# Third layer's attention: outputs built transposed with the values as the stationary operand, and GpSimd's tile work moved to VectorE and ScalarE

## The chip, the cores and the metric

The kernel runs on one core of a Trainium2 chip. A core has TensorE (PE, with the loading of its stationary operand shown as PEld), VectorE (DVE), ScalarE (ACT), GpSimd (POOL) and SyncE (SP), which issues transfers. Each engine takes its own instructions strictly in the order in which the program issued them, and semaphores order the engines among each other. The metric is the device time of one execution in microseconds, lower is better; a time of this kernel is compared by the median of several runs.

## The reference, cut to what matters

The program is three transformer layers on 256 tokens of width 1024. The third layer's attention is a sparse one with 16 heads of 64 in 4 groups; queries of a group share keys and values. With 256 tokens the selected blocks and the window both come to plain causal attention over their own keys and values, so that what the kernel must compute for each head is

```python
s = einsum('qd,kd->qk', q, k_slc) * scale      # selected branch, causal
o_slc = softmax(s) @ v_slc
s = einsum('qd,kd->qk', q, k_win) * scale      # window branch, causal
o_win = softmax(s) @ v_win
p_cmp = softmax(q @ k_cmp.T * scale)           # 15 compressed keys
o_cmp = p_cmp @ v_cmp
o = g[0] * o_cmp + g[1] * o_slc + g[2] * o_win # gates, one per head and branch
x = x + concat(o) @ od_w_out
```

with `q`, the keys and the values projected by `od_w_in` and the keys and queries rotated (rope). All of it is float32. Where a plain float32 product would cost too much, the kernel splits an operand into a rounded part `hi` and a remainder `lo` and uses three products.

## The kernel before, in words

The third layer's attention is the stage in `nsa`, run by `pace(nsa(...), od_fill(), 1.0)`. Its order is written out by hand (`manual_schedule`), so each engine sees the instructions as the program issues them.

`nsa` is a software pipeline over 28 units. A unit with `j` is a block of 128 queries (`j` 0 or 1) for one head of a group (`j` = 1, `hp` = 1) or two (`j` = 0, `hp` = 2), for both branches `s` (selected, window); `par` says whether the heads lie in the lower or the upper 64 partitions. Four units `a` to `d` without `j` are the compressed branch of a group. In step t the program issues `weigh` of the unit two steps back, `turn` of the unit three back, `scores` of the unit t, `values` of the unit four back and `out` of the unit five back, then `pace` takes from `od_fill` about one part of weights.

- `scores`: PE forms the scores (lines 2553 to 2555) in PSUM, DVE takes the row maxima (2557), ACT the exponentials with their sums (2563).
- `weigh`: DVE takes the reciprocal of the sums, multiplies it by the gates (2578, 2579) and scales the probabilities, one `tensor_scalar` for each head and branch (2584).
- `turn`: PE transposes the four 128-column blocks of probabilities (2595); ACT or DVE copies them out of PSUM as `pT` (2598, 2600).
- `values`: PE multiplies with the probabilities `pT` as the stationary operand and 64 columns of values `vsw` as the moving one (2619). The output has queries on its partitions; a bank holds a group's four heads and both query blocks. In the last unit of a query block ACT copies 256 columns to `Onsa` (2523).
- `out`: PE transposes `Onsa` (2628), and `split` writes `mix`: ACT the `hi` part (303), DVE the `lo` part (307).

`od_fill` supplies the layer's own projections (weights in float32 are loaded to `raw`, split by `parts`: `whi` by ACT at line 303 and `wlo` by DVE at line 307 or by POOL at line 305, then multiplied at lines 296 to 298 by `mm3`), the rope of queries and keys, the two compress steps, and the first half of the output projection (`out_pair`). The split of a part is issued up to six parts before its product. From the first step of `nsa` on, `K.pool_share = range(6)` sends every `wlo` of the stage to POOL. POOL also makes the remainders of the rotated queries and keys (`stack`, line 2296; `twice`, line 2305), the shifted upper half of the two compress inputs and the sum with their position term (`upper`, lines 2340 and 2348), and two small products of the compressed branch (2545, 2575). Before step t a unit waits (in program order) until the queries of its group are there, so that `pace` issues as much of `od_fill` as is needed; that makes some steps long.

Of the kernel before, what the change touches and what calls it, by code (L numbers as in the profile page):

```python
# [2290 lines left out]
def stack(K, dst, rows, src, low=None):  # L2291


    nc = K.nc
    nc.scalar.activation(dst[rows], src[rows], AF.Copy)
    nc.gpsimd.tensor_tensor(dst[HIP if rows == LOP else LOP], src[rows], dst[rows].bitcast(F32), op=OP.subtract)


def twice(K, hi, lo, rows, src):
# [4 lines left out]
    for o in (LOP, HIP):  # L2304
        nc.gpsimd.tensor_tensor(lo[o], src[rows], hi[rows].bitcast(F32), op=OP.subtract)


def od_blocks(K, pool, hT, T, done):
# [24 lines left out]
    def halves(c0, m, roped, flag):  # L2333
# [3 lines left out]
        def upper():  # L2337
            dst = T["XC"][m]
            for g in range(0, 4, 2):
                nc.gpsimd.tensor_scalar(dst[HIP, g:g + 2, :255], dst[LOP, g:g + 2, 1:], 1.0, None, op0=OP.mult)  # L2340
# [4 lines left out]
            for g in range(4):  # L2345
                a = dst[:, g, :]
                win = bass.AP(tensor=a.tensor, offset=a.offset, ap=[list(a.ap[0]), [2, 16], [16, 15]])
                nc.gpsimd.tensor_tensor(tmp[:, :, g, :], win, bc(pe, 2, 15), op=OP.add)
# [126 lines left out]
def nsa(K, pool, T, mix, done):  # L2475

    nc = K.nc
# [32 lines left out]
    pos, mixed = {}, []  # L2510

    def into(u):

        new = u.b not in pos
        if new:
            pos[u.b] = bank(K)
        return pos[u.b], new

    def ends(u):
        u.O = {}  # L2520
        for j in u.ends:
            u.O[j] = pool.tile([128, 256], F32, name="Onsa", bufs=2)
            nc.scalar.activation(u.O[j], pos[u.b][:, j * 256:j * 256 + 256], AF.Copy)

    def scores(u):
        b = u.b
        if u.j is None:
# [17 lines left out]
            nc.gpsimd.tensor_tensor(u.sv, u.sv, bc(mv, 2, 16), op=OP.subtract)  # L2545
# [21 lines left out]
    def weigh(u):  # L2567
        if u.j is None:
# [6 lines left out]
            nc.gpsimd.tensor_tensor(u.sv, u.sv, bc(dv, 2, 16), op=OP.mult)  # L2575
# [4 lines left out]
        for ii in range(u.hp):  # L2580
            h = 4 * u.b + 2 * (u.i0 + ii) + u.par
            for s in range(2):
                q = (ii * 2 + s) * u.nk
                nc.vector.tensor_scalar(u.pr[:, q:q + u.nk], u.pr[:, q:q + u.nk], den[:, u.j, h, s:s + 1], None, op0=OP.mult)  # L2584
# [18 lines left out]
    def values(u):  # L2603
        if u.j is None:
            po, new = into(u)
            for j in range(2):
                nc.tensor.matmul(po[:, j * 256:j * 256 + 256], u.pT[:, j * 128:j * 128 + 128],
                                 T["vbd"][:, u.b].rearrange("p h d -> p (h d)"), start=new and j == 0, stop=bool(u.ends),
                                 skip_group_check=True)
            ends(u)  # L2610
            return 0.9
        j, g = u.j, u.b
        po, new = into(u)
        for ii in range(u.hp):
            o = j * 256 + (2 * (u.i0 + ii) + u.par) * 64
            for s in range(2):
# [240 lines left out]
```

## Time and profile before

| | |
|---|---|
| device time, median of 3 runs | 1319.19 us (1313.31 to 1320.64) |
| profiled execution: its own time, and its span | 1319.46 us, 1317.7 us |
| busy over the span: PE, PEld | 1246.6 us (95%), 1076.8 us (82%) |
| DVE, ACT, POOL | 921.5 us (70%), 738.0 us (56%), 295.1 us (22%) |
| mean granted clock of TensorE | 0.97 |
| attention of the third layer | about 949 to 1105 us of the span |

A busy PE is not yet PE at its peak, since matmuls overlap and their ends are modelled: what counts is how far apart their starts are. A busy share is a mean over stages with different limits, so that the stage has to be looked at by itself. A granted clock of 1.0 is 2.4 GHz and of 0.5 is 1.2 GHz; a mean between them is a mix.

### The profile page before, as it was taken

The page shows a single profiled execution, that of the slowest core. Times are in us where ns is not written, and L with a number is a line of the kernel's source. Part 1 is how long each engine was busy: PE and PEld are TensorE (multiplying, and loading weights), DVE is VectorE, ACT ScalarE, POOL GpSimd, SP SyncE. Part 2 cuts the span into 40 slices and gives each one's busy share as a digit, 9 for nine tenths or more (in the row PEclk, how much of TensorE's full clock was granted, in tenths as well). Part 3 has the DMA queues.
Part 4 walks back from the last instruction along what each step waited for, and adds up shares of the span by engine and source line. Part 5 has one row for each costly group of instructions (what it writes and reads, how often), then busy time and mean ns, then how long its engine had stood idle before and what let it go on. Part 6 is the DMA issues. An engine that isn't in the chain of part 4 may idle for free.

```text
span 1317.7 us, 21124 instructions
## 1 busy us (share of the span) xinstructions
PE 1246.6 (95%) x7798; PEld 1076.8 (82%) x7798; DVE 921.5 (70%) x1711; ACT 738.0 (56%) x1545; POOL 295.1 (22%) x332
## 2 busy tenths in 40 slices
PE   7998999799999999989999999999999999999997
PEld 7687997677777777768876799988888777999986
DVE  4778535699999999986866555555468676655562
ACT  6854313489888886865444344454455554544451
POOL 7133005534343432311020000000048321000000
PEclk9999967899999999999999999999999999999999
DMA  8321006669999999737321365565252313555560
GB/s 276 112 96 49 2 1 176 210 236 346 368 325 323 321 355 310 257 110 224 129 65 33 113 192 191 184 224 186 70 159 65 129 33 96 179 176 177 190 224 33
DMA packets 173292, 228.65 MB, mean 174 GB/s; under 512 B 10577, under 2 KB 152225, under 8 KB 173185
## 3 DMA queue, kind: packets, MB, share of 16 engines
q1 hardware_dynamic: 171680, 223.77, 50.7%
q0 software_dynamic: 1504, 3.49, 1.1%
q8 instruction: 63, 1.03, 0.3%
q14 instruction: 45, 0.36, 0.1%
HBM read 226.18 MB, written 1.05 MB: 172 GB/s over the span
## 4 chain that ended last, share of the span: by engine, by line
PE 47%; DVE 4%; ACT 2%; issue 1%; DMA 1%; POOL 0%; DVEq 0%; POOLq 0%; ACTq 0%
PE ps L298 13%; PE ps L296 13%; PE ps L297 13%; PE ps L2619 1%; DMA raw<-in_ev_w_in_dram 1%; DVE pr L2584 1%; PE ps L2595 1%; PE ps L1880 1%; DVE wlo L307 1%; PE ps L2554 1%; PE ps L2197 1%; PE ps L2093 1%; PE ps L2437 1%; ACT whi L303 1%; PE ps L2025 1%
## 5 line engine op out<-in xcount | busy, mean ns | idle before, releaser
L307 DVE TENSOR_TENSOR wlo<-raw,whi 128x512 fp32r<-128x512 f32 (+2 forms) x712 | 514.4, 773 | 75.4 <-ACT whi L303 73.9
L303 ACT ACTIVATE whi<-raw 128x512 fp32r<-128x512 f32 (+1 forms) x821 | 470.7, 624 | 113.6 <-PE ps L298 32.7
L296 PE MATMUL ps<-hTh,whi 128*128 128x256 f32 (+1 forms) x1032 | 301.4, 292 | 1.2 <-ACT whi L303 1.2
L298 PE MATMUL ps<-hTh,wlo 128*128 128x256 f32 (+1 forms) x1032 | 292.3, 283 | 0.2 <-DVE wlo L307 0.2
L297 PE MATMUL ps<-hTl,whi 128*128 128x256 f32 (+1 forms) x1032 | 291.8, 283 | 0.0
L305 POOL TENSOR_TENSOR wlo<-raw,whi 128x512 fp32r<-128x512 f32 x109 | 165.7, 1532 | 302.3 <-ACT whi L303 230.3
L296 PEld LDWEIGHTS ps<-hTh,whi 128*128 128x128 f32 (+1 forms) x1032 | 196.6, 190 | 6.0 <-issue 3.2
L297 PEld LDWEIGHTS ps<-hTl,whi 128*128 128x128 f32 (+1 forms) x1032 | 197.2, 191 | 2.7 <-issue 2.4
L298 PEld LDWEIGHTS ps<-hTh,wlo 128*128 128x128 f32 (+1 forms) x1032 | 195.9, 190 | 0.4 <-DVE wlo L307 0.4
L271 POOL TENSOR_TENSOR nrs<-nv,mhalf 128x1 f32<-128x1 f32 x10 | 5.6, 556 | 469.0 <-DVE nv L1678 469.0
L297 PE MATMUL ps<-wlo,xh 128*128 128x512 f32 x256 | 102.0, 398 | 3.3 <-DVE wlo L307 2.9
L296 PE MATMUL ps<-whi,xh 128*128 128x512 f32 x256 | 103.9, 406 | 0.0
L298 PE MATMUL ps<-whi,xl 128*128 128x512 f32 x256 | 101.0, 395 | 0.0
L303 ACT ACTIVATE hh<-sl 128x512 fp32r<-128x512 f32 x20 | 12.6, 631 | 115.0 <-DVE sl L1770 115.0
L1770 DVE TENSOR_TENSOR sl<-sl,ps 128x512 f32<-128x512 f32 x20 | 13.7, 687 | 88.9 <-PE ps L298 88.9
L296 PE MATMUL ps<-whi,hTh 128*128 128x256 f32 (+3 forms) x192 | 62.6, 327 | 9.5 <-ACT hTh L303 5.5
L297 PE MATMUL ps<-wlo,hh 128*128 128x512 f32 x176 | 69.6, 395 | 0.0
L296 PE MATMUL ps<-whi,hh 128*128 128x512 f32 x176 | 69.3, 394 | 0.0
L298 PE MATMUL ps<-whi,hTl 128*128 128x256 f32 (+3 forms) x192 | 61.7, 322 | 1.3 <-DVE hTl L307 1.3
L297 PE MATMUL ps<-wlo,hTh 128*128 128x256 f32 (+3 forms) x192 | 61.5, 321 | 1.2 <-POOL wlo L305 0.8
L297 PEld LDWEIGHTS ps<-wlo,xh 128*128 128x128 f32 x256 | 48.1, 188 | 16.8 <-DVE wlo L307 7.2
L298 PEld LDWEIGHTS ps<-whi,xl 128*128 128x128 f32 x256 | 48.1, 188 | 11.0
(882 smaller groups left out, 2251.5 us busy)
## 6 DMA issues: line engine op xcount, KB each, us to landing
raw<-in_w_gate_dram SPq DMA_DIRECT2D x64, 512.0 KB, 6.0
raw<-in_w_up_dram SPq DMA_DIRECT2D x64, 512.0 KB, 6.8
raw<-in_w_down_dram SPq DMA_DIRECT2D x32, 1024.0 KB, 7.2
raw<-in_ffn_w_gate_dram SPq DMA_DIRECT2D x22, 1024.0 KB, 5.2
raw<-in_ffn_w_up_dram SPq DMA_DIRECT2D x22, 1024.0 KB, 5.7
raw<-in_ffn_w_down_dram SPq DMA_DIRECT2D x22, 1024.0 KB, 5.0
raw<-in_ev_w_in_dram SPq DMA_DIRECT2D x11, 1024.0 KB, 5.4
raw<-in_od_w_in_dram SPq DMA_DIRECT2D x10, 1024.0 KB, 5.2
```

Of the source, the lines that this page charges most:

```text
L296: nc.tensor.matmul(ps, lh, rh, start=start, stop=False, **kw)
L297: nc.tensor.matmul(ps, lh, rl, start=False, stop=False, **kw)
L298: nc.tensor.matmul(ps, ll, rh, start=False, stop=stop, **kw)
L303: K.nc.scalar.activation(hi, src, AF.Copy)
L305: K.nc.gpsimd.tensor_tensor(lo, src, hi.bitcast(F32), op=OP.subtract)
L307: K.nc.vector.tensor_tensor(lo, src, hi.bitcast(F32), op=OP.subtract)
L1770: nc.vector.tensor_tensor(sl, sl, pu, op=OP.mult)
L1880: nc.tensor.matmul(p2, c[f"R{d}"], z.rearrange("p b t -> p (b t)"), start=True, stop=True)
L2025: nc.tensor.matmul(p[:, bb * nk:bb * nk + nk], T["iqT"][rows[par], b0 + bb, j * 128:j * 128 + 128], ikT[rows[par], :nk], start=True, stop= ...
L2093: nc.tensor.matmul(o, T["qrT"][r, i, js], krT[r, :nk], start=False, stop=False, skip_group_check=True)
L2197: nc.tensor.matmul(oo, qb[rows[m], h0 + i, js], kb[rows[m], h0 + i, :nk], start=i == 0, stop=False, skip_group_check=True)
L2437: nc.tensor.matmul(p[:, :60], w1[:, i, :], tmp[:, i].rearrange("p g n -> p (g n)"), start=i == 0, stop=i == 15)
```

## The change

`values` swaps the operands: 64 columns of `vsw` are stationary and the transposed probabilities move, 128 columns for a unit with `j` = 1 and 256 for one with `j` = 0. The output has the head's 64 value dimensions on partitions, the lower 64 for the heads with `par` 0, the upper 64 for those with `par` 1. A unit with `par` 0 keeps its `pT`; the unit with `par` 1 issues the products of both, in turn. A group's bank then holds what `mix` needs, so that `Onsa`, its copy and the transposes in `out` are gone, `out` splits from the bank itself, and the pipeline is one step shorter. The compressed branch is turned round in the same way.

Nothing of the layer's tile work is left on POOL: `wlo` in this stage, `stack`, `twice`, the position term and the two small products are issued on DVE, the shifted copy on ACT, and of `weigh`'s scalings those of the window branch (`s` = 1) go to ACT.

```diff
@@ stack, twice @@
-    nc.gpsimd.tensor_tensor(dst[HIP if rows == LOP else LOP], src[rows], dst[rows].bitcast(F32), op=OP.subtract)
+    nc.vector.tensor_tensor(dst[HIP if rows == LOP else LOP], src[rows], dst[rows].bitcast(F32), op=OP.subtract)
...
-        nc.gpsimd.tensor_tensor(lo[o], src[rows], hi[rows].bitcast(F32), op=OP.subtract)
+        nc.vector.tensor_tensor(lo[o], src[rows], hi[rows].bitcast(F32), op=OP.subtract)
@@ upper @@
-                nc.gpsimd.tensor_scalar(dst[HIP, g:g + 2, :255], dst[LOP, g:g + 2, 1:], 1.0, None, op0=OP.mult)
+                nc.scalar.activation(dst[HIP, g:g + 2, :255], dst[LOP, g:g + 2, 1:], AF.Copy)
...
-                nc.gpsimd.tensor_tensor(tmp[:, :, g, :], win, bc(pe, 2, 15), op=OP.add)
+                nc.vector.tensor_tensor(tmp[:, :, g, :], win, bc(pe, 2, 15), op=OP.add)
@@ nsa @@
-    def ends(u):
-        u.O = {}
-        for j in u.ends:
-            u.O[j] = pool.tile([128, 256], F32, name="Onsa", bufs=2)
-            nc.scalar.activation(u.O[j], pos[u.b][:, j * 256:j * 256 + 256], AF.Copy)
...
-            nc.gpsimd.tensor_tensor(u.sv, u.sv, bc(mv, 2, 16), op=OP.subtract)
+            nc.vector.tensor_tensor(u.sv, u.sv, bc(mv, 2, 16), op=OP.subtract)
...
-            nc.gpsimd.tensor_tensor(u.sv, u.sv, bc(dv, 2, 16), op=OP.mult)
+            nc.vector.tensor_tensor(u.sv, u.sv, bc(dv, 2, 16), op=OP.mult)
...
-                nc.vector.tensor_scalar(u.pr[:, q:q + u.nk], u.pr[:, q:q + u.nk], den[:, u.j, h, s:s + 1], None, op0=OP.mult)
+                o, d = u.pr[:, q:q + u.nk], den[:, u.j, h, s:s + 1]
+                if s:
+                    nc.scalar.activation(o, o, AF.Copy, scale=d)
+                else:
+                    nc.vector.tensor_scalar(o, o, d, None, op0=OP.mult)
...
         j, g = u.j, u.b
-        po, new = into(u)
-        for ii in range(u.hp):
-            o = j * 256 + (2 * (u.i0 + ii) + u.par) * 64
-            for s in range(2):
-                for b in range(j + 1):
-                    bb = (ii * 2 + s) * (j + 1) + b
-                    nc.tensor.matmul(po[:, o:o + 64], u.pT[:, bb * 128:bb * 128 + 128], vsw[:, b, s, g * 64:g * 64 + 64],
-                                     start=new and ii + s + b == 0, stop=s == 1 and b == j, skip_group_check=True)
-        ends(u)
-        return 0.9
+        if u.par == 0:
+            held[g] = u.pT
+            return 0.0
+        pts = [t.rearrange("p (i s b q) -> p i s b q", i=u.hp, s=2, b=j + 1) for t in (held.pop(g), u.pT)]
+        o = po[:, u.i0:u.i0 + u.hp, u.js]
+        for s in range(2):
+            for b in range(j + 1):
+                for par, r in enumerate(rows):
+                    nc.tensor.matmul(o[r], vsw[:, b, s, g * 64:g * 64 + 64], pts[par][:, :, s, b], start=new[par],
+                                     stop=s == 1 and b == j, skip_group_check=True)
+                    new[par] = False
+        return 0.55
 
     def out(u):
         for j in u.ends:
-            p = bank(K)
-            for k in range(2):
-                nc.tensor.transpose(p[:, k * 128:k * 128 + 128], u.O[j][:, k * 128:k * 128 + 128], K.ident)
             ks, t = slice(2 * u.b, 2 * u.b + 2), slice(j * 128, j * 128 + 128)
-            split(K, mix[0][:, ks, t], mix[1][:, ks, t], p[:, :256].rearrange("p (k t) -> p k t", k=2))
+            split(K, mix[0][:, ks, t], mix[1][:, ks, t], pos[u.b][:, :, t])
...
-    lags = ((weigh, 2), (turn, 3), (scores, 0), (values, 4), (out, 5))
+    lags = ((weigh, 2), (turn, 3), (scores, 0), (values, 4), (out, 4))
...
-        if not t:
-            K.pool_share = range(6)
```

## Rows read from the trace of the kernel before

**Rows 1.** Busy time in stretches of the stage: PE, PEld, DVE, ACT, POOL, clock, DMA.

```profile
988.00:1001.00 13.00, 11.37 (x69) 9.26 (x70) 12.50 (x25) 6.88 (x25) 11.06 (x10) 0.87 0.29 83
...
sum 169.00, PE 160.80 PEld 134.13 DVE 122.62 ACT 92.03 POOL 68.56; mean PE 12.37 PEld 10.32 DVE 9.43 ACT 7.08 POOL 5.27
```

**Rows 2.** PE's instructions grouped, 955 to 1115 us: busy us, mean ns.

```profile
L2619 PE MATMUL ps<-vsw,pT 128*128 128x64 f32 x192 | 24.2, 269 | 0.0
```

**Rows 3.** Chain that ended last, in order of time: start, us, what.

```profile
995.98 0.84 PE ps L2619 x8
...
1084.21 0.44 PE ps L2628 x4
```

**Rows 4.** PE in order of time, layer two's output projection (L2155 alternates halves).

```profile
717.34 1.09 PE L2155 MATMUL ps<-olT,wuv 128*64 128x128 f32 x16
...
727.59 0.40 PE L297 MATMUL ps<-wlo,mxh 128*128 128x512 f32 x1
727.92 0.66 PE L2155 MATMUL ps<-olT,wuv 128*64 128x128 f32 x8
728.50 0.50 PE L298 MATMUL ps<-whi,mxl 128*128 128x512 f32 x1
728.84 0.40 PE L296 MATMUL ps<-whi,mxh 128*128 128x512 f32 x1
729.07 0.40 PE L297 MATMUL ps<-wlo,mxh 128*128 128x512 f32 x1
```

**Rows 5.** DVE's instructions grouped by shape, 949 to 1115 us.

```profile
L307 DVE TENSOR_TENSOR wlo<-raw,whi 128x512 fp32r<-128x512 f32 x30 | 21.7, 775 | 12.0 <-ACT whi L303 11.9
L2584 DVE TENSOR_SCALAR pr<-pr,den 128x256 f32<-128x256 f32 x32 | 18.3, 612 | 0.9
L2584 DVE TENSOR_SCALAR pr<-pr,den 128x128 f32<-128x128 f32 x32 | 12.7, 459 | 0.3
```

**Rows 6.** POOL's instructions grouped by shape, same stretch.

```profile
L305 POOL TENSOR_TENSOR wlo<-raw,whi 128x512 fp32r<-128x512 f32 x24 | 30.6, 1293 | 29.7 <-ACT whi L303 23.5 <-issue 6.0
L2305 POOL TENSOR_TENSOR KTl<-kf,KTh 64x512 fp32r<-64x512 f32 x8 | 11.8, 1476 | 26.8 <-ACT KTh L2303 26.5
```

**Rows 7.** DVE in order of time, four places of the stage.

```profile
984.17 0.67 DVE L307 TENSOR_TENSOR wlo<-raw,whi 128x512 fp32r<-128x512 f32 x1
984.77 1.27 DVE L2557 TENSOR_REDUCE mx<-ps 128x2 f32<-128x512 f32 x2
...
988.36 1.63 DVE L2584 TENSOR_SCALAR pr<-pr,den 128x256 f32<-128x256 f32 x2
...
1010.30 0.69 DVE L2557 TENSOR_REDUCE mx<-ps 128x2 f32<-128x512 f32 x1 [1.76 <-PE ps L2555]
...
1013.95 0.69 DVE L2557 TENSOR_REDUCE mx<-ps 128x2 f32<-128x512 f32 x1 [0.19 <-PE ps L2555]
...
1053.10 0.61 DVE L2584 TENSOR_SCALAR pr<-pr,den 128x256 f32<-128x256 f32 x2
...
1094.31 3.92 DVE L2584 TENSOR_SCALAR pr<-pr,den 128x128 f32<-128x128 f32 x4
```

**Rows 8.** POOL in order of time, around two of those places.

```profile
988.51 2.65 POOL L305 TENSOR_TENSOR wlo<-raw,whi 128x512 fp32r<-128x512 f32 x2 [6.01 <-issue]
...
1092.99 4.97 POOL L305 TENSOR_TENSOR wlo<-raw,whi 128x512 fp32r<-128x512 f32 x4 [4.79 <-ACT whi L303]
```

**Rows 9.** Who waited for whom, 955 to 1110 us: total, times, longest.

```profile
ACT pr L2563 <- DVE mx L2557: 20.0, 17, 3.8
...
ACT s L2546 <- POOL s L2545: 8.0, 4, 3.6
...
PE ps L2595 <- DVE pr L2584: 7.1, 8, 1.5
```

**Rows 10.** ACT in order of time, one unit's exponentials and the split behind them.

```profile
986.84 0.47 ACT L2563 ACTIVATE pr<-ps,mx 128x256 f32<-128x256 f32 x1
...
987.75 0.62 ACT L303 ACTIVATE whi<-raw 128x512 fp32r<-128x512 f32 x1
```

More of the change, by code (lines that the diff above doesn't have):

```diff
@@ L2509, in nsa @@
             [u for u in g if u.j == 1][-1].ends = (1,)
-    pos, mixed = {}, []
+    pos, fresh, mixed, held = {}, {}, [], {}
     def into(u):
[L2514 to L2517, printed above, removed]
-    def ends(u):
-        u.O = {}
-        for j in u.ends:
-            u.O[j] = pool.tile([128, 256], F32, name="Onsa", bufs=2)
-            nc.scalar.activation(u.O[j], pos[u.b][:, j * 256:j * 256 + 256], AF.Copy)
+        if u.b not in pos:
+            pos[u.b] = bank(K).rearrange("p (i t) -> p i t", i=2)
+            fresh[u.b] = [True, True]
+        return pos[u.b]
     def scores(u):
@@ L2603, in values @@
     def values(u):
+        po = into(u)
+        new = fresh[u.b]
         if u.j is None:
-            po, new = into(u)
[L2606 to L2609, printed above, removed]
-            ends(u)
-            return 0.9
-        j, g = u.j, u.b
@@ L2613, in values @@
-        po, new = into(u)
-        for ii in range(u.hp):
-            o = j * 256 + (2 * (u.i0 + ii) + u.par) * 64
-            for s in range(2):
-                for b in range(j + 1):
-                    bb = (ii * 2 + s) * (j + 1) + b
-                    nc.tensor.matmul(po[:, o:o + 64], u.pT[:, bb * 128:bb * 128 + 128], vsw[:, b, s, g * 64:g * 64 + 64],
-                                     start=new and ii + s + b == 0, stop=s == 1 and b == j, skip_group_check=True)
-        ends(u)
-        return 0.9
+            for i in range(2):
+                nc.tensor.matmul(po[:, i], T["vbd"][:, u.b, 2 * i:2 * i + 2].rearrange("p h d -> p (h d)"), u.pT,
+                                 start=new[0] and i == 0, stop=bool(u.ends), skip_group_check=True)
@@ new lines, in values @@
+            new[:] = False, False
+            return 0.5
+        j, g = u.j, u.b
+        if u.par == 0:
[9 more added lines that the diff above has]
+                    new[par] = False
@@ L2632, in out @@
                 mixed.append(("mix", u.b))
-        return 0.2 * len(u.ends)
-    lags = ((weigh, 2), (turn, 3), (scores, 0), (values, 4), (out, 5))
+        return 0.0
+    lags = ((weigh, 2), (turn, 3), (scores, 0), (values, 4), (out, 4))
     yield lambda: done.issuperset(("ks", "kw"))
-    for t in range(len(units) + 5):
+    for t in range(len(units) + 4):
         if t < len(units):
             yield lambda: units[t].b in done and (units[t].j is not None or "cmp" in done)
-        if not t:
-            K.pool_share = range(6)
@@ L2642, in nsa @@
         done.update(mixed)
         yield sum(f(units[t - d]) or 0.0 for f, d in lags if 0 <= t - d < len(units))
-    K.pool_share = ()
     done.update(mixed)
```

## The prediction, as it was made before the result

> **What bounds the kernel now.** I read the page first: PE is busy nearly throughout, so time can leave only where PE's own work shrinks or PE stands still. Next the busy time by stretches of the stage that the change touches [rows 1]: of 169 us PE is busy 160.8, DVE 122.6, ACT 92.0 and POOL 68.6. PE bounds the stage as a mean, but not everywhere: from 988 to 1001 DVE is busy 12.5 of 13 us, PE only 11.4, and PE's granted clock falls to 0.87, a mix of 2.4 and 1.2 GHz. The list of waits says for what PE stands still: for DVE's scaling of the probabilities, 7.1 us in eight times [rows 9].
>
> Then DVE in order of time, beside POOL. Two scalings of 256 columns take 0.61 us at 1053, when POOL has nothing; at 988 they take 1.63, at 1094 four of half that length take 3.92, both while POOL works on `wlo` [rows 7, 8]. So DVE's scalings, on average 612 and 459 ns [rows 5], are long because of POOL. The Trainium skill (SBUF — State Buffer, "SBUF: two separate sides") says that GpSimd and a VectorE instruction that reads two SBUF tensors, or runs in a two-port mode, hold a shared port pair exclusively. The trace agrees with that by the 1.63 and 3.92 us.
>
> **PE's work.** The old `values` is 192 instructions [rows 2] (each float32 product counts as two) in 24 runs of eight at 0.84 us, so 20.2 us; `out` has four runs of four transposes at 0.44, so 1.8 [rows 3]. Together 22.0.
>
> The new form does not occur in this stage, but layer two's L2155 has it: 128 rows, 64 output columns, lower and upper half in turn, 128 moving columns. Sixteen of them span 1.09 us and eight 0.66 [rows 4]: eight more cost 0.43, or 0.054 each, half of what a lone stream of 128 columns in two passes would be if the halves did not overlap. Of the 12 new runs, eight (`j` = 1) have 16 instructions of 128 columns, 0.86 us; four (`j` = 0) have 8 of 256 columns, by length 0.108 each and also 0.86. Sum 10.4.
>
> Each run also leaves the full-array form and comes back to it. In layer two, starts of full 512-column products lie 0.23 us apart (728.84 to 729.07); with a run of eight between them 0.91 (727.59 to 728.50), so 0.91 − 0.23 − 0.43 = 0.25 us is lost around the run, and the next start is another 0.34 − 0.23 = 0.11 late [rows 4]. I take 0.36, 12 times 4.3 us; the lower end is 0.25, or 3.0. The Trainium skill speaks against the change here: a change of tiling mode drains the engine (TensorEngine Tiling (Array Packing), "Key Properties"). It gives no price; the trace's 0.25 to 0.36 us is what such a drain would be, and without one the part below would be 4.3 us better.
>
> New sum 14.7, so PE loses 7.3 us of work. Bounds: 8.6 with the cheap entry; if the halves did not overlap, 20.7 + 4.3 = 25.0 and PE gains 3.0. The compressed branch has the same number of products of 256 columns as before: nothing. I leave it there, since the halves overlap in every run of L2155.
>
> **DVE's and ACT's work.** Moved to DVE: 24 `wlo` [rows 6], 8 key remainders of the same length [rows 6] and, by the code, 8 query remainders too: 40 at 0.60 us, the distance between starts at 984.17 and 984.77 [rows 7], 24.0. Eight position sums of 240 columns at about half, 2.4, and eight small products, at most 0.2 each, 1.6. Sum 28.0. Taken off: half of the 64 scalings, at most 0.3 each without POOL, 8 to 9 us; and the time lost to POOL, 32 × (612 − 300) + 32 × (459 − 300) ns = 15.1 us (half of that is in the moved ones, but would have gone either way), and from each of 30 `wlo` 775 − 670 ns (670 at 984.17, with POOL idle), 3.2 [rows 5, 7]. DVE comes to 122.6 + 28.0 − 9 − 18 = 124 us: no relief in total, but no load either. ACT gains 32 scalings, at most 0.47 each by an exponential of 256 columns, and 4 shifted copies of 510 columns, by `whi` about 0.6 each [rows 10], and loses eight copies of 256 columns, about 0.4 each: 92 + 15 + 2.4 − 3 = 106. Both are hidden under PE's 160.8 − 7.3 as sums. ACT's 8.0 us of waits for POOL in the compressed branch [rows 9] shrink with it. No transfer is added, and none is issued behind the moved work; a `raw` buffer is free sooner where POOL's 1.29 us per `wlo` was last.
>
> **What the move costs in order.** `wlo` on POOL waits for `whi` by itself: 23.5 us in all [rows 6]. On DVE it stands in line, and what is behind it waits too: the next unit's reciprocal, its scaling, its copy of `pT`, its maximum. In a step with a part of weights the engines then hand over in a ring: DVE's maximum 0.64 (half of 1.27 at 984.77), ACT's two exponentials 0.91 (986.84 to 987.75), `whi` 0.52 (0.62 to its end), DVE's `wlo` 0.60, reciprocal and gates about 0.4, scaling 0.3, and every other unit a copy of 0.6 [rows 7, 10]: 3.7 us, near 4 with the hand-offs. Today's maxima are 3.65 us apart at 1010.30 and 1013.95, both behind PE [rows 7]; PE's new step would be 3.65 − 7.3/24 = 3.35. So in such a step DVE, not PE, sets the pace and loses 0.3 to 0.7 us. The moved remainders of queries and the two shifted copies with their position sums stand in the same line, 2 us each. The scaling of one unit is wanted by `turn` only one step later: that is the cover, one step; when it is used up, PE waits at 2595. From 984 to 1035 about 13 steps are of this kind, and DVE falls behind by 4 to 6 us; the two compress steps, PE work with nothing for DVE, give some back. I charge PE 4.0 us there, with 0 (the cover suffices) and 13 × (0.91 + 0.52 − 0.4) = 13 (no cover, only the reciprocal overlapped) as ends.
>
> From 1040 on there are nine `wlo`, all in the two bursts of the output projection. There the scalings become short: at 1094 3.92 us become two of about 0.3 plus four `wlo` in line, 3.0; of PE's 7.1 us of standing for line 2584 I take 3.0 as gone, and 1.0 for the copy `Onsa` and its handing over at the end of groups: 4.0, ends 0 and 8.1.
>
> **Sum.** −7.3 + 4.0 − 4.0 = −7.3. From the profiled execution's own 1319.46 us (1317.7 of span and 1.8 around it, 0.3 above the median of 1319.19) that is 1312.2; I say 1312. Clock: the 0.87 stretch lies where PE stands still; as I let PE stand there as before, I give nothing back for it, at most 13 × 0.13 = 1.7 us for each such stretch.
>
> **Rivals.**
> - The cover suffices: the ring costs nothing, all of the 7.1 us and the 1.0 go, PE saves 8.6, one stretch of low clock with them: 1319.5 − 8.6 − 8.1 − 1.7 = 1301. For it: the fill is split up to six parts ahead, so PE seldom needs a `wlo` at once. Against it: 2584 stands behind `wlo`.
> - It evens out: the ring costs what PE saves, 7 to 9 us instead of 4, with the other 4 gained: 1316 to 1319. For it: from 988 to 1001 DVE is full already [rows 1].
> - Slower: the ring sets the pace. ACT's window scaling waits for DVE's reciprocal and stands before the next exponentials, so that both engines wait for each other in every step; ACT waits 20.0 us for DVE's maxima even now [rows 9]. At 13 us in the first half and another 4 in the out-projection's bursts, with PE's 7.3 saved: 1319.5 + 17 − 7.3 = 1329. It decides against the change once the ring costs over 11.3 us.
> - The halves do not overlap, or overlap only in short runs: PE's 7.3 becomes −3.0, 1322 with the rest as forecast.
>
> **Numbers.** About 0.5%, 6.6 us, is what a measurement of this kernel can tell from no change. Chances: forecast (1306 to 1317) 0.45, the cover suffices 0.25, evens out 0.17, the ring sets the pace 0.10, no overlap 0.03. Faster than 1312.6: all of the second and half of the first, 0.48. Slower than 1325.8: 0.10. Within: 0.42. The range leaves out the far half of the fast case and the slow one: 1299 to 1323.
>
> **What would show it.** In the changed profile: 160 instructions at the new `values`, two starting almost together, 0.11 us a pair, and no transposes in `out`; scalings of 256 columns near 0.3 us on DVE; POOL empty between 950 and 1105; DVE's idle before `wlo` for `whi` up from 11.9 us [rows 5]. PE's idle before the transposes of `turn` tells the rivals apart: near zero in the fast case, some 8 us by the forecast (moved to before 1035), over 15 in the slow one. I am wrong if DVE's line never reaches PE, or if the clock drops more often because PE is fed in shorter bursts.

## The result: measurably slower, and the profile after

Over 16 runs of each in turn on one chip, the kernel before took 1315.13 us (median) and the changed kernel 1321.51: a ratio of 1.0059 with a 95% interval of 1.004 to 1.0079. One of the changed kernel's 16 runs took 2382.15 us and is left out of the ratio, as is every run in such a slow state. The forecast was 1312 us, a gain. The profiled execution spans 1323.1 us.

Of each profile I take the length of **the stage**, from ScalarE's first rounding of a key (L2303) to the first transposes of the layer's last norm (L1691). What follows it takes 200.0 to 200.2 us in every profile; what precedes it takes 951 to 967 us and differs with the clock in layer one between executions of one kernel, so spans of single profiles are not compared. The stage took 156.0 us before and 168.7 after, of which 10.2 and 30.7 at 1.2 GHz (summed from the trace's clock records). That difference, 12.7, is more than the 7.8 us of the ratio: one profile of a stage can stand some 5 us off its kernel's median, so verdicts go by the ratios.

The stretches of the changed kernel that answer to [rows 1] (busy us of PE, PEld, DVE, ACT, POOL with counts, PE's clock, DMA share, GB/s):

```profile
975.00:988.00 13.00, 8.93 (x44) 6.27 (x43) 7.67 (x16) 7.03 (x18) 0.00 (x0) 0.77 0.50 144
988.00:1001.00 13.00, 11.88 (x86) 9.70 (x86) 8.04 (x21) 7.72 (x28) 0.00 (x0) 0.96 0.07 19
...
1079.00:1092.00 13.00, 10.32 (x41) 6.81 (x42) 7.99 (x24) 3.72 (x14) 0.00 (x0) 0.74 0.27 83
...
sum 169.00, PE 147.54 PEld 113.86 DVE 116.00 ACT 96.78 POOL 0.00; mean PE 11.35 PEld 8.76 DVE 8.92 ACT 7.44 POOL 0.00
```

In these stretches, which [rows 1] has at the same times of the span, PE is busy 13.3 us less than before. But the stage lies elsewhere in them, at 961.5 to 1117.5 us before and at 954.2 to 1122.9 after, so that loads are better compared over the stage itself. There PE is busy 148.1 us before and 147.3 after, part of the latter at half clock, and stands 21.5 us where it stood 7.9; DVE goes from 113.0 to 115.9 and ACT from 86.2 to 98.8. No other engine is full in any stretch: nothing is overloaded, the engines wait for each other. The groups that changed, by shape (busy us, mean ns, idle before and what ended it), beside [rows 2, 5]:

```profile
L307 DVE TENSOR_TENSOR wlo<-raw,whi 128x512 fp32r<-128x512 f32 x45 | 29.2, 688 | 20.2 <-ACT whi L303 19.8
...
L2621 PE MATMUL ps<-pT,vsw 128*64 128x128 f32 x128 | 10.5, 316 | 0.0
...
L2582 ACT ACTIVATE pr<-pr,den 128x256 f32<-128x256 f32 x16 | 8.1, 507 | 13.5 <-DVE den L2575 13.5
...
L2621 PE MATMUL ps<-pT,vsw 128*64 128x256 f32 x32 | 6.1, 516 | 0.0
L2584 DVE TENSOR_SCALAR pr<-pr,den 128x256 f32<-128x256 f32 x16 | 5.7, 353 | 0.6
...
L2584 DVE TENSOR_SCALAR pr<-pr,den 128x128 f32<-128x128 f32 x16 | 3.9, 284 | 0.3
```

The scalings are short now (612 and 459 ns became 353 and 284), as the Trainium skill's rule on the shared port pair (SBUF — State Buffer, "SBUF: two separate sides") would have it with GpSimd silent; the values have the 160 instructions that were foreseen. What grew is the first row's last column: DVE stands 19.8 us for `whi`. The waits, beside [rows 9] (total, times, longest):

```profile
ACT pr L2582 <- DVE den L2575: 22.7, 14, 3.9
DVE wlo L307 <- ACT whi L303: 19.8, 11, 2.9
...
ACT pr L2559 <- DVE mx L2553: 14.4, 15, 3.0
PE ps L2595 <- DVE pr L2584: 11.6, 8, 4.1
...
PE ps L2590 <- DVE s L2571: 6.5, 2, 5.3
```

They wait in a ring: each stands for the next, and the last for the first. DVE at the stage's first units, then ACT, then PE, each in order of time (start, length, idle before):

```profile
976.04 0.69 DVE L2553 TENSOR_REDUCE mx<-ps 128x2 f32<-128x512 f32 x1
979.67 0.69 DVE L307 TENSOR_TENSOR wlo<-raw,whi 128x512 fp32r<-128x512 f32 x1 [2.94 <-ACT whi L303]
980.28 0.68 DVE L2553 TENSOR_REDUCE mx<-ps 128x2 f32<-128x512 f32 x1
982.57 0.69 DVE L307 TENSOR_TENSOR wlo<-raw,whi 128x512 fp32r<-128x512 f32 x1 [1.61 <-ACT whi L303]
983.18 0.16 DVE L2574 RECIPROCAL den<-den 128x2 f32<-128x2 f32 x1
```

```profile
976.80 1.28 ACT L2559 ACT_TABLE_LOAD   x1 [3.06 <-DVE mx L2553]
978.10 0.47 ACT L2559 ACTIVATE pr<-ps,mx 128x256 f32<-128x256 f32 x1
...
979.01 0.62 ACT L303 ACTIVATE whi<-raw 128x512 fp32r<-128x512 f32 x1
981.00 0.47 ACT L2559 ACTIVATE pr<-ps,mx 128x256 f32<-128x256 f32 x1 [1.36 <-DVE mx L2553]
...
981.91 0.62 ACT L303 ACTIVATE whi<-raw 128x512 fp32r<-128x512 f32 x1
```

```profile
978.97 1.02 PE L1880 MATMUL ps<-rz,cst_b 128*128 128x512 f32 x2
984.07 1.09 PE L2595 MATMUL ps<-cst_i,pr 128*128 128x128 f32 x4 [4.07 <-DVE pr L2584]
984.81 0.78 PE L2549 MATMUL ps<-KTh,q 128*128 128x512 f32 x1
```

The second unit's scores were complete at 976.83 (their last product, L2551, starts at 976.55 and takes 0.28), but its maxima start at 980.28, behind a `wlo` that waits for a `whi` that stands on ACT behind the first unit's exponentials. ACT in turn stands for those maxima. So two units that could overlap go one after the other, the reciprocal starts at 983.18, PE stands 4.07 us, and right behind that its clock has fallen: a 512-column product takes 0.78 us, in stretches at 2.4 GHz 0.39 to 0.48. Transfers are no rival here: ACT's only stand for one is 1.0 us in the changed kernel's stage and 4.1 before.

### The profile page after: what moved, and what is told of

It is laid out like the page before. It is cut to its first block, busy times and chain, and to the rows that moved or that the text cites. A ratio compares the mean times of both kernels' runs of the same rounds, so it can differ in the third digit from the quotient of the medians.

```text
span 1323.1 us, 20988 instructions
## 1 busy us (share of the span) xinstructions
PE 1237.9 (94%) x7750; PEld 1059.8 (80%) x7750; DVE 924.6 (70%) x1735; ACT 750.8 (57%) x1573; POOL 228.5 (17%) x272
## 3 DMA queue, kind: packets, MB, share of 16 engines
q8 instruction: 62, 1.02, 0.3%
## 4 chain that ended last, share of the span: by engine, by line
PE 45%; DVE 6%; ACT 3%; DMA 1%; issue 1%; POOL 0%; DVEq 0%; POOLq 0%; ACTq 0%
PE ps L296 12%; PE ps L298 12%; PE ps L297 12%; DVE wlo L307 2%; DMA raw<-in_ev_w_in_dram 1%; PE ps L2621 1%; ACT pr L2559 1%; PE ps L1880 1%; PE ps L2197 1%; PE ps L2093 1%; ACT whi L303 1%; PE ps L2437 1%; PE ps L2025 1%; PE ps L2595 1%; PE ps L2092 0%
## 5 line engine op out<-in xcount | busy, mean ns | idle before, releaser
L307 DVE TENSOR_TENSOR wlo<-raw,whi 128x512 fp32r<-128x512 f32 (+2 forms) x736 | 527.5, 767 | 87.6 <-ACT whi L303 85.6
L305 POOL TENSOR_TENSOR wlo<-raw,whi 128x512 fp32r<-128x512 f32 x85 | 135.8, 1605 | 262.0 <-ACT whi L303 203.9
L303 ACT ACTIVATE hh<-sl 128x512 fp32r<-128x512 f32 x20 | 12.6, 632 | 115.0 <-DVE sl L1770 115.0
L297 PEld LDWEIGHTS ps<-wlo,xh 128*128 128x128 f32 x256 | 48.5, 190 | 17.3 <-DVE wlo L307 7.4
```

Of the source, the lines that this page charges most:

```text
L297: nc.tensor.matmul(ps, lh, rl, start=False, stop=False, **kw)
L303: K.nc.scalar.activation(hi, src, AF.Copy)
L305: K.nc.gpsimd.tensor_tensor(lo, src, hi.bitcast(F32), op=OP.subtract)
L307: K.nc.vector.tensor_tensor(lo, src, hi.bitcast(F32), op=OP.subtract)
```

## The experiments

All 17 runs, with the kernel before run beside them: ratio to it, median, and from one profile the stage and its time at 1.2 GHz. "Columns" is the new form of the values, "rows" the old one. A low part is the remainder that is left when an operand is rounded, `wlo` for the weights and line 2296 for the queries; "POOL" and "DVE" say which engine makes it. The profiles of runs 6 and 11 come from their slowest executions (1336.65 and 1324.75 us).

| run | values | weights' low parts | queries' | other | ratio (95%) | us | stage | at 1.2 GHz |
|---|---|---|---|---|---|---|---|---|
| before | rows | POOL | POOL | | 1 | 1315.1 | 156.0 | 10.2 |
| changed | columns | DVE | DVE | | 1.0059 (1.004 to 1.0079) | 1321.5 | 168.7 | 30.7 |
| 1 | columns | POOL | POOL | no other move | 1.0022 (0.9996 to 1.0048) | 1317.7 | 163.5 | 34.1 |
| 2 | rows | DVE | DVE | | 1.0152 (1.0121 to 1.0184) | 1334.2 | 175.1 | 44.4 |
| 3 | columns | POOL | DVE | | 0.9999 (0.9968 to 1.003) | 1314.8 | 158.5 | 30.7 |
| 4 | columns | DVE | DVE | all scalings on DVE | 1.0111 (1.0062 to 1.016) | 1329.0 | 173.7 | 51.2 |
| 5 | columns | POOL | DVE | dummy products | 1.0001 (0.9977 to 1.0025) | 1313.9 | 158.3 | 10.2 |
| 6 | columns | DVE, late | DVE | loads late too | 1.0066 (1.0033 to 1.0099) | 1324.9 | 173.4 | 54.6 |
| 7 | columns | POOL | DVE | half the fill a step | 1.0042 (1.0011 to 1.0073) | 1320.0 | 164.1 | 34.1 |
| 8 | columns | POOL | DVE | halves in turn | 0.9987 (0.9959 to 1.0015) | 1313.1 | 157.5 | 17.1 |
| 9 | rows | POOL | DVE | | 1.0069 (1.0032 to 1.0107) | 1324.5 | 165.1 | 37.5 |
| 10 | columns | DVE, late | DVE | | 0.9999 (0.9959 to 1.004) | 1317.4 | 160.6 | 27.3 |
| 11 | columns | POOL | POOL | | 0.997 (0.9942 to 0.9998) | 1312.8 | 155.4 | 17.1 |
| 12 | rows | POOL | POOL | | 0.9961 (0.9934 to 0.9987) | 1311.4 | 151.6 | 3.4 |
| 13 | columns | POOL | POOL | halves in turn | 0.995 (0.9923 to 0.9977) | 1312.0 | 154.5 | 10.2 |
| 14 | rows | POOL | POOL | all scalings on DVE | 1.0018 (0.9994 to 1.0043) | 1318.4 | 161.6 | 17.1 |
| 15 | columns | POOL | POOL | `out` a step later | 0.9975 (0.9941 to 1.0009) | 1313.2 | 158.2 | 23.9 |
| 16 | columns | DVE | POOL | | 1.0041 (1.0008 to 1.0073) | 1321.1 | 164.0 | 30.7 |

Where a difference of two ratios is given in us, it is times 1315. Maxima are counted from 0 and timed from the stage's start.

**Run 1, the values alone**: line 2621 and all that hangs on it as changed, every `nc.gpsimd` back, all scalings on DVE.

> The values transposed, all tile work on the engines of before. The stage (from the first rounded key on ScalarE to the first transposes of the last layer's norm) took 156.0 us before and 168.7 after the change. Ring theory (VectorE's remainder waits in line behind ScalarE's exponentials): this half of the change is sound, TensorE saves its 7 us, stage 147 to 152, total 4 to 9 us under the kernel before. Form theory (the new runs drain TensorE and lower its clock): stage over 160, total at least 4 us over the kernel before.

Not faster, and both forecasts missed in part: the stage of 163.5 us is over the form theory's 160, the time, 2.9 us over the kernel before, under the 4 us of that theory and far from the ring theory's gain. Until the 19th maxima it keeps step with the kernel before (99.4 us against 99.2); from there it takes 44.9 us to the 27th, much of it at 1.2 GHz, against 29.4. Not all of that is loss: with the values in columns 19.2 us of the stage are left behind the 27th maxima, before 27.4.

**Run 2, the moves alone**: the kernel before with each `nc.gpsimd` of the diff replaced, `pool_share` left out and the window branch's scalings on ACT.

> The moves off GpSimd alone, the values as before. Ring theory: the stage is longer than with the whole change, as TensorE's 7 us are not saved: 172 to 178, total 12 to 20 us over the kernel before. Form theory: the moves are harmless, the stage is near 156 or a few us under it.

The slowest of all: the loss lies in the moves. Next, which of them.

**Run 3, the weights' low parts back on GpSimd.**

```diff
+        if not t:
+            K.pool_share = range(6)
...
+    K.pool_share = ()
```

> The whole change, but the remainders of the weights go to GpSimd again in this stage. If the remainder of the weights in VectorE's line is the ring: stage 148 to 156, total below the kernel before. If ScalarE's scalings, which wait for VectorE's gates, are the ring: stage still over 162. A middle result, 156 to 162, says that both close it.

This one move is 0.6% (7.9 us); the stage of 158.5 us is the middle result, which was to mean that both close the ring. The 12th maxima come at 79.3 us, in the changed kernel at 90.9, before at 83.1.

**Run 4, all scalings on DVE again.**

```diff
-                if s:
-                    nc.scalar.activation(o, o, AF.Copy, scale=d)
-                else:
-                    nc.vector.tensor_scalar(o, o, d, None, op0=OP.mult)
+                nc.vector.tensor_scalar(o, o, d, None, op0=OP.mult)
```

> The whole change, but VectorE scales the window branch's probabilities again. If ScalarE's scalings are the ring (it stood 22.7 us for VectorE's gates in the changed kernel): stage under 160. If the weights' remainder in line is: stage 165 to 171, within 3 us of the changed kernel, as VectorE only gets some 9 us more to do.

0.5% slower than the changed kernel (1.0111 against 1.0059, about as much as the two intervals can tell): the scalings on ACT are no part of the loss, the list of waits notwithstanding, where their 22.7 us stand first.

**Run 5, run 3 with more for TensorE**: six products of 256 bfloat16 columns into an unused bank in each step from the 12th.

> The changed kernel with the weights' remainders on GpSimd (158.5 us of stage, TensorE at 1.2 GHz for 30.7 us of it, against 10.2 before), plus work that nobody needs: six products of 256 bf16 columns at the head of each step from the thirteenth on, where no projection is left to fill TensorE. It computes nothing of the output. Clock theory (TensorE, fed less after the change, falls to its lower clock and loses there what the shorter runs save): the low stretches shrink to under 14 us, stage 148 to 153, total at least 4 us under the kernel before, although TensorE has some 12 us more to do. Rival (waits for VectorE set the time, the clock only follows them): the stage grows by up to 5 us or stays.

The clock holds (10.2 us low, as before) and the time does not move. Six dummy products take 0.67 us, in twenty steps 13 us of PE's time. Either PE's time is free there, as run 8 will show for 4 us of it, or the dummies eat what the clock gives: this run alone doesn't tell half clock's part in run 3.

**Run 6, low parts on DVE behind the next maxima**, issued from a list at the end of a step. The raw loads behind them went late too: ACT stood 8.1 us for one. It tells nothing on the order; run 10 repeats it.

> The changed kernel, with VectorE's remainder of a weight part issued one step later, behind the next unit's maxima, so that it no longer waits for ScalarE's exponentials; nothing on GpSimd. Ring theory: as good as with the remainders on GpSimd, stage 155 to 160, total 5 to 9 us under the changed kernel. Rival (VectorE has too much to do, whatever the order): stage within 4 us of 168.7.

**Run 7, run 3 with `pace(..., 0.5)`.**

> Remainders on GpSimd as in the second run above of that kind, and half as much of the projections taken per step (0.5 for 1.0), so that some are left for the steps after the twelfth. Clock theory: low stretches shorter, stage 148 to 156. Rival: the late projections delay the compressed branch and the last queries, stage over 160.

Spreading the fill over more steps cost 0.4%, about as much as the two intervals can tell.

**Run 8, run 3 with the two half columns one after the other** (the loop over `par` outermost).

> Remainders on GpSimd, and the transposed outputs with all products of the lower half first, then those of the upper one, so that the halves do not overlap: some 10 us more of TensorE's time. If the overlapping form itself lowers the clock: low stretches near 10 us, stage 156 to 162. If the clock falls because TensorE is fed less: stretches shorter than 30.7 too, as the same work fills more time, so this run alone does not part these two; if they stay at 30 the work is not what decides. Without any clock effect: stage 166 to 169.

No slower. (The busy time that this adds was over-estimated: it is 4 us, below.) At least these 4 us of TensorE's work are not what run 3's steps wait for.

**The kernel before once more**, for what one profile is worth.

> The kernel before, unchanged, profiled a second time: what one profile of the stage (first rounded key to the first transposes of the last norm) can be trusted for. If one profile stands for the kernel: 156.0 us within 1.5, with 10.2 us at the low clock within 5. If the low clock in the stage comes and goes from one execution to the next: over 20 us at the low clock and a stage of over 158, and then the 30 to 55 us at the low clock of the changed kernels may not be put down to their edits.

156.4 and 10.2 us, as the first time: the low clock of the changed kernels is taken for their edits' from here on, though each of them was profiled once.

**Run 9, the moves but the weights' low parts, old values.**

> The values in the old form, with every move off GpSimd but that of the weights' low parts, which stay on GpSimd. Theory (the low parts in VectorE's line cost the stage some 10 us, and the column form of the values buys nothing since TensorE isn't what the steps wait for): as the changed kernel with the low parts on GpSimd, 1313 to 1317 us, ratio 0.997 to 1.002, and the 12th maxima at about 79.5 us after the stage's start as there (83.1 before). Rival (the column form does give its 7 us, and the other moves cost them): slower than that kernel by about 5 us, 1319 to 1322, ratio 1.003 to 1.006.

The rival, and more than it said: 9 us slower than run 3. So here the columns are worth 0.7%, though they were worth nothing by themselves in run 1. The stretch after the 13th maxima shows why (fields as in the first block):

```profile
1039.00:1052.00 13.00, 13.00 (x60) 12.13 (x60) 7.04 (x23) 5.73 (x19) 0.00 (x0) 0.50 0.00 1
1052.00:1065.00 13.00, 13.00 (x52) 10.50 (x51) 6.02 (x25) 5.15 (x23) 0.00 (x0) 0.50 0.00 0
```

PE is full, at 1.2 GHz: 37.5 us in one spell. At half clock PE's work sets the pace, and the form with less of it wins. What started the spell is the next question; in all kernels with the queries' low parts on DVE the 13th maxima come 5.1 to 7.2 us after the 12th (in eight of ten 5.1 to 5.5), in all with them on POOL 2.6 to 3.0.

**Run 10, run 6 with the loads where they were.**

```diff
-                        self.K.late.append((None, self.load))
+                        settle(self.K)
+                        self.load()
```

`settle` issues the low parts that are owed; the load follows.

> The changed kernel with each low part of a weight issued on VectorE behind the next step's maxima, not between them, and with the raw weights' loads where they were (an earlier form of this run held them back too). Theory (the cost is the order on VectorE's line: maxima behind low part behind ScalarE's high part behind ScalarE's exponentials): most of the 10 us come back, the 12th maxima at 80 to 84 us (90.9 in the changed kernel, 79.3 with the low parts on GpSimd), 1314 to 1317 us. Rival (it is VectorE's added work as such, 45 low parts of 0.69 us): the 12th maxima stays at 88 to 91 us, and the time at 1320 to 1323.

By the ratio this has all of run 3's gain with the work still on DVE: 0.9999. In the profile the 12th maxima come at 84.6, so that some half of run 3's lead is there. Its DVE and PE at the first units:

```profile
977.19 0.69 DVE L2579 TENSOR_REDUCE mx<-ps 128x2 f32<-128x512 f32 x1
978.04 0.69 DVE L2579 TENSOR_REDUCE mx<-ps 128x2 f32<-128x512 f32 x1 [0.17 <-PE ps L2577]
980.82 0.69 DVE L369 TENSOR_TENSOR wlo<-raw,whi 128x512 fp32r<-128x512 f32 x1 [2.09 <-ACT whi L359]
```

```profile
983.75 0.63 PE L2621 MATMUL ps<-cst_i,pr 128*128 128x128 f32 x4 [2.57 <-DVE pr L2610]
984.13 0.48 PE L2575 MATMUL ps<-KTh,q 128*128 128x512 f32 x1
```

The second maxima come 0.85 us after the first (4.24 in the changed kernel), PE stands 2.57 instead of 4.07 us, and its clock is still up behind that (0.48). The step after is longer: the third maxima start at 983.51, 6.32 us behind the first (7.80 in the changed kernel), then PE stands another 2.29 us, and there its clock falls, at 989.1. So the late order loosens the ring and doesn't undo it. What the weights' low parts cost by the ratio is their place in the line, not the work.

**The step before run 9's spell.** PE stands 1.77 us for the scaling there, and 1.5 us later it is at half clock. Run 3 has the same step, with DVE and PE as follows:

```profile
1039.66 0.68 DVE L1883 TENSOR_TENSOR qf<-ps,qf 128x512 f32<-128x512 f32 x1
1041.40 1.39 DVE L2296 TENSOR_TENSOR q<-qf,q 64x512 fp32r<-64x512 f32 x2 [1.06 <-ACT q L2295]
1042.80 0.18 DVE L2574 RECIPROCAL den<-den 128x4 f32<-128x4 f32 x1
```

```profile
1043.64 0.65 PE L2595 MATMUL ps<-cst_i,pr 128*128 128x128 f32 x4 [1.95 <-DVE pr L2584]
...
1045.69 1.39 PE L2595 MATMUL ps<-cst_i,pr 128*128 128x128 f32 x4 [0.43 <-DVE pr L2584]
```

It is the same ring with the query's low part in place of the weight's: DVE waits for ACT's rounding, the reciprocals stand behind it, PE stands 1.95 us, and two microseconds later four transposes take 1.39 us instead of 0.65.

**Runs 11 to 14, the queries' low parts back on GpSimd too** (`nc.gpsimd` in line 2296), with run 3, run 9, run 8, and run 12 with the scalings on DVE.

> The changed kernel with the low parts of both the weights and the queries on GpSimd (the KTl low parts, the window sums, the compressed scores and the scalings stay where the change put them). In all kernels with the queries' low parts on VectorE the 13th maxima come 5.1 to 5.5 us after the 12th, in both with them on GpSimd 2.9 to 3.0; in the first, VectorE stands for ScalarE's q rounding ahead of the reciprocals that TensorE's transposes need, TensorE stands 1.95 us, and its clock falls to half. Theory (that stand starts the spell at half clock): that step is 3 us again, under 20 us at the low clock, a stage of 150 to 155 us (158.5 with only the weights' low parts back), 1306 to 1312 us, ratio 0.994 to 0.998. Rival (the clock falls anyway since the column form feeds TensorE less in each step, as where only the values were changed, 34 us at the low clock): 27 to 35 us low, a stage of 155 to 159, 1312 to 1316 us.

> The same placement with the values in the old form. Theory (the stand over the queries starts the spell at half clock, and the old form of the values keeps TensorE fed as before): about 10 us at the low clock, the 12th maxima at 80 us and the rest as before, a stage of 152 to 154 us, 1309 to 1313 us, ratio 0.995 to 0.999, faster than before. Rival (ScalarE's added scalings and copies set the pace of the last steps, as with only the weights' low parts back, where they ran at 4 us a step): over 30 us at the low clock, a stage of 160 to 165, 1319 to 1325 us.

> As the first kernel of this call, with the two half columns one after the other and not side by side, some 10 us more of TensorE's work in the stage, which at half clock was no slower. Theory (what TensorE is given in the bare steps matters by the clock alone): at most 17 us at the low clock and no slower than the first kernel, within 2 us of it. Rival (at full clock TensorE's work counts again): slower than the first kernel by 4 to 8 us.

> As the second kernel of this call, with the scalings of the probabilities all on VectorE again. If ScalarE's share of the scalings is a link in the steps (VectorE's reciprocal, ScalarE's scaling behind its exponentials, TensorE's transposes): faster than the second kernel by 1 to 4 us. If it only takes work off VectorE, as undoing it under the full change made the stage 5 us longer: slower by 2 to 5 us.

The step is 2.6 us again (3.0 in run 14), and runs 11, 12 and 13 beat the kernel before, by 0.3, 0.4 and 0.5%, and so the changed one too. Run 12, with the old values, has 3.4 us at 1.2 GHz; its sum over 948 to 1104 us, and a stretch to set beside run 9's:

```profile
1039.00:1052.00 13.00, 12.36 (x94) 10.41 (x94) 11.30 (x36) 8.19 (x27) 2.19 (x2) 1.00 0.00 1
...
sum 156.00, PE 149.44 PEld 123.77 DVE 108.49 ACT 99.55 POOL 41.74; mean PE 12.45 PEld 10.31 DVE 9.04 ACT 8.30 POOL 3.48
```

The queries' low parts alone cost 1.1% with the old values (run 9 against 12), which half clock hits harder, and 0.3% with the columns (3 against 11). With both on GpSimd, where the profiles have only 17.1 and 3.4 us at half clock, the columns are worth nothing (0.997 against 0.9961; 7.3 us would be 0.0056, outside what the two intervals allow). Run 14 is 0.6% slower than run 12: the scalings on ACT are the change's gain, some 7 us, as run 4 had said. What PE stands for in run 12 and, last line, in run 14:

```profile
PE ps L2599 <- DVE pr L2588: 3.0, 4, 1.5
PE ps L2599 <- ACT pr L2586: 1.9, 2, 1.1
...
PE ps L2594 <- DVE s L2575: 0.5, 1, 0.5
```

```profile
PE ps L2596 <- DVE pr L2585: 9.5, 9, 2.6
```

With the scalings shared it stands 4.9 us for them, with all on DVE 9.5. The columns' own busy time, in run 11 and, halves in turn, in run 13:

```profile
L2621 PE MATMUL ps<-pT,vsw 128*64 128x128 f32 x128 | 8.8, 279 | 0.0
L2621 PE MATMUL ps<-pT,vsw 128*64 128x256 f32 x32 | 5.2, 456 | 0.0
```

```profile
L2621 PE MATMUL ps<-pT,vsw 128*64 128x128 f32 x128 | 12.7, 279 | 0.0
L2621 PE MATMUL ps<-pT,vsw 128*64 128x256 f32 x32 | 5.3, 455 | 0.0
```

14.0 us, in turn 18.0, against 24.2 in the old form [rows 2]. These sums count the last product of every run to its end; the forecast counted from a run's start to the next product's. Run 11's PE around one run of sixteen:

```profile
1038.76 0.28 PE L2551 MATMUL ps<-causb,identb 128*128 128x256 bf16 x1
1038.97 1.09 PE L2621 MATMUL ps<-pT,vsw 128*64 128x128 f32 x16
1039.99 0.39 PE L296 MATMUL ps<-hTh,whi 128*128 128x256 f32 x1
```

From 1038.76 to 1039.99 are 1.23 us; the mask's product is followed after 0.12 elsewhere (978.85 to 978.97 in the changed kernel) and sixteen products are 0.86, so 0.25 are lost. Counted like that, at 2.4 GHz, a run takes 1.11 to 1.12 us (1.02 to the next start, 0.09 more than elsewhere before it), twelve 13.4, against 20.2 for the old 24. With `out` PE is spared 8.6 us, the forecast's better end. But the halves do not overlap as it took them to. In turn, a run of sixteen products of 128 columns takes 1.51 us to the next start instead of 1.02, which is less than double, and a run of eight of 256 columns the same 1.02 in both orders.

But run 13 gives 4.0 of it back and is no slower. Where the columns' saving stays, one place could be read. PE stands 5.6 us for a compressed unit's `s` in run 11, 5.2 in run 13, and 0.5 in run 12 (the third line above). Run 13's longest such stand (DVE, POOL, PE):

```profile
1066.59 0.28 DVE L2566 TENSOR_REDUCE dc<-s 128x8 f32<-128x128 f32 x1
1066.90 0.68 DVE L2567 TENSOR_SCALAR dc<-dc 128x8 f32<-128x8 f32 x1
...
1067.85 0.95 DVE L2569 TENSOR_TENSOR dc<-dc,gts 128x8 f32<-128x8 f32 x1
1068.83 1.31 DVE L2571 TENSOR_TENSOR s<-s,dc 128x128 f32<-128x128 f32 x1
```

```profile
1066.28 6.22 POOL L305 TENSOR_TENSOR wlo<-raw,whi 128x512 fp32r<-128x512 f32 x5 [22.33 <-ACT whi L303]
```

```profile
1070.29 0.61 PE L2590 MATMUL ps<-cst_i,s 128*64 128x128 f32 x2 [4.44 <-DVE s L2571]
```

The output projection's five low parts fall on a compressed unit's small operations (0.17 us where POOL is silent), and PE stands 4.44 us.

**Run 15, run 11 with `out` a step later** (`(out, 5)` in `lags`), to move that burst. **Run 16, the queries' low parts alone on GpSimd.**

> As the kernel with the column form and the low parts of weights and queries on GpSimd (1312.8 us), with the split of a finished group one step behind its values, as the old form had it, and not in the same step. In the column form the output projection's five ScalarE roundings and the five GpSimd low parts behind them (6.2 us) fall on the normalising of a compressed unit, whose five small VectorE operations take 0.28 to 1.31 us each, and TensorE stands 4.4 us; in the old form they fall one step elsewhere. Theory (that place in the order is where the column form loses what it saves): the step from the 21st to the 22nd maxima falls from 7.4 to 4 or 5 us, the stage to 150 to 153 us, 1308 to 1311 us, ratio 0.993 to 0.996. Rival (the burst meets some other chain of VectorE's and costs the same): no faster than that kernel, 1311 to 1314.

> The changed kernel with only the queries' low parts back on GpSimd, the weights' on VectorE. Taking back the weights' alone gave 0.6% of the time, taking back the queries' after them another 0.3%. If the two add up: ratio 1.002 to 1.004, 1318 to 1321 us. If the queries' stand is hidden as long as the weights' low parts hold the line: no change, 1.005 to 1.007. If the queries' stand is what starts the low clock, and the weights' low parts cost only with it: 0.997 to 1.000.

In run 15 the step to the 22nd maxima fell from 7.4 to 4.5 us and the next grew from 2.7 to 6.2: the rival was right, the burst meets another chain. PE's stands for `s` fell to 3.1 us, and the time stayed. Run 16: as if the two add up, 0.2% for the queries' here (1.0041 against 1.0059), 0.3% in run 11 against run 3; each of these is within the intervals, the 1.1% of run 12 against run 9 is not.

## Why the prediction was wrong, step by step

- **What the move costs in order: the step that failed.** The ring was seen, its parts were right, and it was charged 4.0 us (about 13 steps at 0.3 to 0.7, one step of cover), with 13 us as the end without cover. Taking both low parts off DVE's line gives 0.9970 against 1.0059, 11.7 us, and 25.1 in the old form (run 2 against 12). Run 10 shows for the weights' that it is the order. The error lay in the cover: it was counted for the scaling, which is wanted a step later, while the next unit's *maxima* also stand behind `wlo` and have no cover. Each such step is then a whole round: maxima to maxima 4.24 us at 976.04, table load included, and 3.56 at 980.28, where the late order took 0.85 and then 5.47. From the first to the 12th maxima the profiles have 69.0 us in the changed kernel, 59.9 before, 62.8 in run 10 and 57.5 in run 3, so that the changed kernel loses 9.1 us there against the kernel before and 11.5 against run 3: near the forecast's end without cover. The queries' remainders were named at "2 us each" and then priced with the rest; at one place alone they made PE stand 1.95 us.
- **The rival "the ring sets the pace"** had the right direction, and a wrong link: it named ACT's window scaling, which run 4 clears. Its threshold of 11.3 us, beyond which the change loses, is met within the uncertainty of the 11.7.
- **PE's work: right as a size, wrong as time.** 8.6 us were spared against 7.3 forecast; entering and leaving a run costs 0.25 us, in the 0.25 to 0.36 that the Trainium skill's drain (TensorEngine Tiling (Array Packing), "Key Properties") was taken for. The forecast's worst case without overlap, 25.0 us, was too dark: with the halves in turn the twelve runs take 17.3. But the sum took the 7.3 us off the end as if they stood apart from the ring. With the clock mostly up they bring nothing (runs 11 to 13); at half clock, where PE is full, 0.7 to 0.9% (run 9 against 3, run 2 against the change, 12.2 us).
- **Waits gone, −4.0: in part, and only without the ring.** Run 12 has 3.0 us of PE's standing for DVE's scalings and 1.9 for ACT's instead of 7.1 [rows 9], so 2.2 are gone of the 3.0 that were forecast for them; the changed kernel 11.6, where the forecast had "some 8" and the slow rival "over 15".
- **The output projection's bursts** were booked as gain. PE's longest stand in the changed kernel is there: 5.34 us until 1081.68 (L2590 in the waits above), while DVE makes five `wlo` in line, 3.10 us from 1076.66 on, ahead of a compressed unit's small operations. With the weights' low parts on POOL the longest stand for `s` was 1.1 us (run 3) to 4.4 (run 11), so how much of it the move made stays open.
- **Clock: "give nothing back".** The spells at 1.2 GHz grew from 10.2 to 30.7 us, and those shown here (the changed kernel's first, run 3's, run 9's) start behind a stand of PE that the ring made. A clock that drops more often was named as a sign of being wrong, with shorter bursts as its reason. Runs 11 and 12 take the stands away, and the low time shrinks to 17.1 and 3.4 us. But the clock is not only a follower: once it is low, PE's work is on the path (run 9). What it costs by itself no run parts from the stands.
- **Loads: right.** By the sums DVE was to gain some 1 us and ACT 14; over the stage they gained 2.9 and 12.6, though single terms were off: scalings 353 ns (0.3 forecast), position sums 570 ns (0.3). Neither load mattered; but the scalings' move to ACT, booked only as load hidden under PE, is the part that pays, 0.5 to 0.6% (runs 4 and 14). That PE's mean load would set the end was the assumption behind both errors, the ring's and PE's.

That 1321.5 us lies inside the forecast's 1299 to 1323 is no merit: the range was built on one execution of 1319.46 us, 4.3 above the later median of the kernel before, and on a gain.

The account by ratios, in us: both low parts +11.7; the scalings −7.5 (run 12 against 14); columns with the clock mostly up +1.2 (run 11 against 12); the other moves +2.4 (run 14); together +7.8, the measured loss. It closes by construction, each term is uncertain by some 4 to 5, and it depends on the order in which the parts are put in: with the columns last it reads low parts +25.1, columns −12.2, the rest as above. The two belong together, since the columns pay where the ring has lowered the clock. Shown are the cost of the low parts and the gain of the scalings; that the columns' saving is lost to other chains of DVE is shown at one place (runs 13 and 15) and for the rest stays open. Also open is why run 1, with nothing moved, loses its clock at the 20th step: PE stands 1.12 us for a compressed unit's product on GpSimd just before, but a like stand of 1.14 us in run 11 (1066.22) is followed by no spell.

## What to carry to other kernels

A piece of work that needs no one's attention belongs on an engine whose line nobody else stands in, even if it is slow there: GpSimd's low part of 1.29 us was the cheaper one, VectorE's of 0.69 us cost a round of the ring, because it stood, behind a wait, ahead of the next unit's maxima. Before moving an operation, write down what stands behind it in the new line, and whether what it waits for stands behind work that needs that very line; if it must move, issue it behind the next thing that the other engines need. And take an engine's saved time off the end only where the waits, not the busy shares, say that it comes last.

## What was not expected of the hardware

- A row of PE can read 13.00 of 13.00 us busy at half clock, in a spell of 37.5 us (run 9): a full engine is no sign that it is fed as before, and work that is free at 2.4 GHz (run 13) is on the path there.
- Two operations of 8 columns on DVE took 0.68 and 0.95 us instead of 0.17 while GpSimd went through five low parts; the reduction and the reciprocal beside them kept their 0.28 and 0.20. As the rows read, an operation that meets GpSimd's loses some 0.5 to 1 us whatever its length (before, two scalings of 256 columns took 1.63 instead of 0.61, four of 128 columns 3.92 [rows 7] instead of the 0.87 at 1043.81), so a chain of small ones is hit hardest.
- Two half-array products side by side gain only where they are short: 0.055 us each from start to start instead of 0.087 with 128 columns, 0.10 in both orders with 256 (runs 11 and 13).
